# Local attention: the scores of both key blocks laid into one 128x128 matrix, and one transpose per query block and head instead of two

## The chip, the cores and the metric

The kernel runs on one core of one Trainium2 chip. The metric is the device time of one execution in microseconds; the median of three runs of the kernel before is 2232.43 us (2231.8 to 2232.46). A core has five engines that run their own instruction streams: TensorE (PE in the profile, its weight loads PEld), VectorE (DVE), ScalarE (ACT), GpSimd (POOL) and SyncE (SP). TensorE writes to PSUM only; VectorE and ScalarE read PSUM and SBUF; DMA queues move data between HBM and SBUF.

## The reference

One decoder layer on 2048 tokens of width 1024. A root-mean-square norm and one wide projection feed three branches: A, an RWKV-7 recurrence with 8 heads of 64; B, causal sliding-window attention with 8 query heads and 2 key/value heads of 64; C, cross-attention into 256 memory tokens. Each branch is gated, projected to 1024 and weighted by a sigmoid gate; the sum goes through an output projection and is added to the input. The change is in branch B, whose core is:

```
qb = q.reshape(bsz, nb, BLOCK, SW_KV_HEADS, SW_GROUP, SW_HEAD_DIM)    # BLOCK = WINDOW = 128
kband, vband = band(k), band(v)            # previous block of 128 keys, then the own block
s = einsum('bnqhgd,bnkhd->bnhgqk', qb, kband) * scale
rel = qi - kj + BLOCK                      # qi in 0..127, kj in 0..255
allowed = (rel >= 0) & (rel < WINDOW)      # and not the padding ahead of block 0
s = where(allowed, s, -1e30)
p = softmax(concatenate([s, sink]))[..., :-1]
o = einsum('bnhgqk,bnkhd->bnqhgd', p, vband)
```

For query qi of a block the allowed keys are those of the previous block with index above qi, and those of the own block with index up to qi. Of the 256 keys in the band exactly 128 are allowed, and each of the 128 column indices is allowed in exactly one of the two blocks (in the first block of the sequence the previous keys are padding).

## The kernel before

The tokens are worked in four blocks of 512 (`TB`), called blocks 0 to 3 here. In each block two generators are interleaved: `stream_r` (branch A: preparation, a triangular inverse on VectorE, a chain of small matmuls) and `stream_f` (cross-attention, then local attention by `swa_kv` and four calls of `swa_pair`, with gates and merges between). Then follow the merge of branch A and the output projection (`output`). Almost all of TensorE's time goes to dense projections, in which a float32 product is made of three float32r products of 128x512 (`gemm3`, lines 467 to 469, and lines 1222 to 1224 in `output`).

The order on each engine isn't the order in which the code is written. All instructions are recorded, and a list scheduler (`steps`, `lay_out`, `order`) places them engine by engine by rank, by estimated costs and by whether a buffer is free; buffers of one tag are taken in program order. The tag `g2` holds 128x512 float32 tiles, `NG` = 11 of them; PSUM has two buffers each of the tags `mm`, `rw` and `as_`, and one each of `oo` and `yps`.

`swa_pair(j, sb, ...)` treats two query heads and four query blocks of 128 tokens. It is called 16 times in all. Its steps:

- Scores (line 1136): for each query block and head, two matmuls of 128x256 (keys split into a high and a low part) into PSUM, the previous block's keys in columns 0 to 127 and the own block's in 128 to 255.
- Line 1140, on VectorE: adds the mask `amask` (0 or -1e30) to 128x256 scores, writes them to SBUF (`prs`) and takes the row's maximum. Eight per pair, each followed by a read of the accumulator.
- Line 1152, on ScalarE: exponential of 128x256 with the row's sum, eight per pair.
- Line 1164, on VectorE: the rows are scaled by the reciprocal sum, eight of 128x256.
- Line 1168: 128x128 transposes on TensorE into an `as_` tile, two for each query block and head, 16 per pair (14 in block 0, whose first query block has no previous keys). Line 1170, on ScalarE: copy of the 128x512 tile to SBUF, four per pair.
- Line 1178: value matmuls, for each query block, key block and head, 128 keys by 64 channels, into the `oo` tile.

`output` (lines 1214 to 1230) multiplies the merged sum by the output weights in two halves `n` of 512 columns. The sum's high parts are eight `g2` tiles (`split_acc`), which live until the second half is done. In each half four PSUM tiles `op[tt]` (two `mm`, two `as_`) collect 24 matmuls each. For each, a `g2` tile `xr` is loaded with the residual rows (line 1228, on ScalarE's DMA queue), line 1229 adds the product on VectorE, and line 1230 stores the tile (the same queue).

Of the kernel before, what the change touches and what calls it, by code (L numbers as in the profile page):

```python
# [9 lines left out]
F32 = mybir.dt.float32  # L10
F32R = mybir.dt.float32r
BF16 = mybir.dt.bfloat16
I32 = mybir.dt.int32
AF = mybir.ActivationFunctionType
# [6 lines left out]
NG = 11  # L21
# [286 lines left out]
def build(tc, A, nsb=4):  # L308
# [19 lines left out]
    def g2(dt=F32, shape=(128, TB)):  # L328
        return gp_.tile(list(shape), dt, name="g2")
# [9 lines left out]
    def s_ps():  # L339
        return ps.tile([128, 512], F32, name="as_", bufs=2)  # L340
# [54 lines left out]
    amask = bp.tile([128, 256], BF16, name="amask")  # L395
# [667 lines left out]
    vt = bp.tile([128, 5, 128], F32, name="Vt")  # L1063

    def swa_kv(sb, hT):
# [31 lines left out]
        S.activation(vt[:, 1:].rearrange("p a b -> p (a b)"), pt, AF.Copy)  # L1097

    def swa_pair(j, sb, hT, yh, yl):
# [29 lines left out]
        for b0 in (0, 2):  # L1129
            prs += [g2(shape=(128, 2, 256)) for _ in range(2)]  # L1130
            sp = [s_ps().rearrange("p (b k) -> p b k", b=2) for _ in range(2)]
            for b in (b0, b0 + 1):
                m0 = m0s[b]
                for i in range(2):
                    for n, kk in enumerate((kH, kL)):
                        PE.matmul(sp[i][:, b - b0, m0:], qs[i][:, b * 128:(b + 1) * 128], kk[:, g, b * 128 + m0:b * 128 + 256], start=n == 0, stop=n == 1)
            for b in (b0, b0 + 1):
                m0 = m0s[b]
                for i in range(2):
                    V.tensor_tensor_reduce(prs[b][:, i, m0:], sp[i][:, b - b0, m0:], amask[:, m0:], 1.0, -3e38, ALU.add, ALU.max, mx[:, b, i:i + 1])  # L1140
# [8 lines left out]
        for b in range(4):  # L1149
            m0 = m0s[b]  # L1150
            for i in range(2):
                S.activation(prs[b][:, i, m0:], prs[b][:, i, m0:], AF.Exp, scale=r2[:, b, i:i + 1], bias=mx[:, b, i:i + 1],  # L1152
                             accum_out=mx[:, b, 2 + i:3 + i])
# [6 lines left out]
        for b in range(4):  # L1160
            m0 = m0s[b]
            kb0 = m0 // 128
            for i in range(2):
                V.tensor_scalar(prs[b][:, i, m0:], prs[b][:, i, m0:], dn[:, b, i:i + 1], None, op0=ALU.mult)
            pt = s_ps().rearrange("p (a k q) -> p a k q", a=2, k=2)
            for i in range(2):
                for kb in range(kb0, 2):
                    PE.transpose(pt[:, i, kb], prs[b][:, i, kb * 128:(kb + 1) * 128], ident)
            P_ = g2(shape=(128, 2, 2, 128))
            last = S.activation(P_[:, :, kb0:], pt[:, :, kb0:], AF.Copy)  # L1170
            Ps.append(P_)
        ops_ = o_ps()
        prev = None
        for b in range(4):
            kb0 = m0s[b] // 128
            for kb in range(kb0, 2):
                for i, h in enumerate((EV, OD)):
                    m = PE.matmul(ops_[h, b * 128:(b + 1) * 128], vt[:, b + kb, g * 64:(g + 1) * 64], Ps[b][:, i, kb], start=kb == kb0, stop=kb == 1)  # L1178
                    behind(m, prev or last, not prev)
                    prev = m  # L1180
# [51 lines left out]
    def masks():  # L1232
        for t, n in ((gmask, "gmask"), (amask, "amask")):
            full = g2()[:, :t.shape[1]]
            nc.sync.dma_start(full, A[n])
            G.tensor_copy(t, full)
# [133 lines left out]
def host(inputs):  # L1370
# [30 lines left out]
    A["gmask"] = np.where(cI < 64, pI % 64 < cI, pI % 64 <= cI - 64).astype(f)  # L1401
    kj = np.arange(256)[None, :]
    A["amask"] = np.where((kj > pI) & (kj <= pI + 128), 0.0, -1e30).astype(f)
# [25 lines left out]
```

## Time and profile before

| | |
|---|---|
| median of three runs | 2232.43 us (2231.8 to 2232.46) |
| span of the profiled execution, first to last instruction | 2231.6 us |
| TensorE busy, weight loads busy | 2210.5 us (99%), 1798.2 us (81%) |
| VectorE busy | 1544.4 us (69%) |
| ScalarE busy | 920.2 us (41%) |
| GpSimd busy | 132.9 us (6%) |
| DMA moved | 433.17 MB, mean 194 GB/s |

The page gives the profiled execution's own time as its span alone; the three timed runs lie 0.2 to 0.9 us above it. The profile names an instruction by its source line, engine and operation, then output <- inputs, then the shapes. "Idle before" is the time in which an engine stood still ahead of an instruction, with the one that released it. A matmul's length includes its way through the array, so lengths of successive matmuls overlap; what one costs is read from the starts.

### The profile page before, as it was taken

To read this page: it belongs to the slowest core of one execution; us is meant where nothing else is said; L and a number is where in the kernel's file an instruction comes from. 1 tells how busy PE (TensorE), PEld (TensorE's weight loads), DVE (VectorE), ACT (ScalarE), POOL (GpSimd) and SP (SyncE) were. 2 spreads that over 40 slices of the span, in tenths; PEclk is the share of its full clock that TensorE was granted. 3 is DMA by queue.
4 is the path that set the end of the run, shared out by engine and by line. 5 is a ranking of instruction groups with operands and counts; after the bars stand their busy time and mean duration, and the time that the engine had idled before them with its cause. 6 is when DMAs were issued, how large, how long until landed. Compare 5 with 4: busy or idle time off the path is not lost. (4 is left out here: it accounts for less than half of the span.)

```text
span 2231.6 us, 36859 instructions
## 1 busy us (share of the span) xinstructions
PE 2210.5 (99%) x13682; PEld 1798.2 (81%) x13682; DVE 1544.4 (69%) x3993; ACT 920.2 (41%) x2042; POOL 132.9 (6%) x193
## 2 busy tenths in 40 slices
PE   8999999999999999999999999999999999999999
PEld 7888778778888778878888878877888887887887
DVE  7799699775479688943438958975245896896312
ACT  6664565445253355423215335432223434534210
POOL 1000010000000010000000001000000001000000
PEclk9999999999999999999999999999999999999999
DMA  6877556679845434446764534445675444344555
GB/s 218 293 240 258 186 183 217 224 274 351 313 163 167 143 133 158 146 169 231 243 237 143 178 125 150 144 142 199 222 254 198 162 156 156 119 151 132 201 196 189
DMA packets 149874, 433.17 MB, mean 194 GB/s; under 512 B 16704, under 2 KB 24256, under 8 KB 149696
## 3 DMA queue, kind: packets, MB, share of 16 engines
q1 hardware_dynamic: 133568, 401.45, 53.0%
q10 hardware_dynamic: 16128, 29.37, 3.9%
q8 instruction: 109, 1.79, 0.3%
q14 instruction: 69, 0.57, 0.1%
HBM read 334.81 MB, written 95.94 MB: 193 GB/s over the span
## 5 line engine op out<-in xcount | busy, mean ns | idle before, releaser
L467 PE MATMUL mm<-hH,whl 128*128 128x512 f32 x1888 | 752.4, 399 | 0.1
L469 PE MATMUL mm<-hH,whl 128*128 128x512 f32 x1888 | 750.2, 397 | 0.0
L468 PE MATMUL mm<-hL,whl 128*128 128x512 f32 x1888 | 745.3, 395 | 0.0
L469 PEld LDWEIGHTS mm<-hH,whl 128*128 128x128 f32 x1888 | 355.1, 188 | 71.8 <-issue 1.5
L467 PEld LDWEIGHTS mm<-hH,whl 128*128 128x128 f32 x1888 | 355.3, 188 | 68.7 <-DVE carry L677 0.4
L468 PEld LDWEIGHTS mm<-hL,whl 128*128 128x128 f32 x1888 | 355.3, 188 | 68.0 <-issue 0.9
L449 ACT ACTIVATE whl<-raw 128x512 fp32r<-128x512 f32 x178 | 111.3, 629 | 151.3 <-PE mm L469 95.1
L450 DVE TENSOR_TENSOR whl<-raw,whl 128x512 fp32r<-128x512 f32 x178 | 122.5, 691 | 48.2 <-ACT whl L449 45.9
L467 PE MATMUL mm<-yh,whl 128*128 128x512 f32 x384 | 151.9, 396 | 1.3 <-ACT gt L1190 0.8
L468 PE MATMUL mm<-yl,whl 128*128 128x512 f32 x384 | 151.1, 393 | 0.0
L469 PE MATMUL mm<-yh,whl 128*128 128x512 f32 x384 | 150.2, 391 | 0.0
L912 ACT ACTIVATE SP<-Z,Pl 64x64 f32<-64x64 f32 x256 | 76.4, 337 | 117.1 <-DVE Z L924 115.5
L819 DVE STREAM_SHUFFLE ibc<-Nc 128x496 f32<-128x496 f32 (+30 forms) x248 | 114.0, 473 | 0.0
L1205 DVE SCALAR_TENSOR_TENSOR g<-g,mm 128x512 f32<-128x512 f32 x32 | 21.8, 682 | 128.3 <-PE mm L469 128.3
L820 DVE TENSOR_TENSOR ibc<-ibc,Yi 128x496 f32<-128x496 f32 (+30 forms) x248 | 104.9, 423 | 4.1
L821 DVE TENSOR_TENSOR Yi<-Yi,ibc 128x496 f32<-128x496 f32 (+30 forms) x248 | 103.5, 418 | 1.2
L924 DVE SCALAR_TENSOR_TENSOR Z<-rw,Pl,SP 64x64 f32<-64x64 f32 x224 | 63.4, 283 | 40.6 <-PE rw L923 37.1
L1190 ACT ACTIVATE gt<-mm 128x512 f32<-128x512 f32 x64 | 37.9, 592 | 118.3 <-PE mm L469 118.2
L467 PEld LDWEIGHTS mm<-yh,whl 128*128 128x128 f32 x384 | 72.2, 188 | 16.9 <-ACT gt L1190 1.2
L468 PEld LDWEIGHTS mm<-yl,whl 128*128 128x128 f32 x384 | 72.2, 188 | 14.6
L1152 ACT ACTIVATE g<-g,mxs,st 128x256 f32<-128x256 f32 (+1 forms) x128 | 74.5, 584 | 22.8 <-DVE mxs L1145 22.6
L469 PEld LDWEIGHTS mm<-yh,whl 128*128 128x128 f32 x384 | 72.2, 188 | 14.4
(1847 smaller groups left out, 3804.7 us busy)
## 6 DMA issues: line engine op xcount, KB each, us to landing
whl<-k SPq DMA_DIRECT2D x486, 512.0 KB, 3.3
k<-whl SPq DMA_DIRECT2D x162, 512.0 KB, 4.3
raw<-in_w_in SPq DMA_DIRECT2D x118, 256.0 KB, 3.2
g<-in_x ACTq DMA_DIRECT2D x32, 256.0 KB, 4.9
out<-g ACTq DMA_DIRECT2D x32, 256.0 KB, 4.3
raw<-in_w_proj SPq DMA_DIRECT2D x24, 256.0 KB, 3.1
rt<-in_x ACTq DMA_DIRECT2D x24, 256.0 KB, 5.2
rt<-in_xt ACTq DMA_DIRECT2D x24, 256.0 KB, 5.5
```

Of the source, the lines that this page charges most:

```text
L449: S.activation(w[:, 0], raw, AF.Copy)
L450: V.tensor_tensor(w[:, 1], raw, w[:, 0].bitcast(F32), op=ALU.subtract)
L467: PE.matmul(out, lh, rh, start=i == 0, stop=False)
L468: PE.matmul(out, lh, rl, start=False, stop=False)
L469: PE.matmul(out, ll, rh, start=False, stop=i == n - 1)
L819: V.stream_shuffle(bc[:, :, :w], N_[:, :, s + 1:], [s] * 32)
L820: V.tensor_tensor(bc[:, :, :w], bc[:, :, :w], Y[:, :, s:s + 1].to_broadcast([128, n, w]), op=ALU.mult)
L821: V.tensor_tensor(Y[:, :, s + 1:], Y[:, :, s + 1:], bc[:, :, :w], op=ALU.add)
L912: S.activation(SP[h, i], Z[h, i, e, c], AF.Copy, scale=g[4][h, c:c + 1])
L924: upds = [V.scalar_tensor_tensor(Sst[h, g[0]] if c == NC_ - 1 else Z[h, i, e, c + 1], pS[h, i, e], g[4][h, c:c + 1], SP[h, i], op0=ALU.mul ...
L1152: S.activation(prs[b][:, i, m0:], prs[b][:, i, m0:], AF.Exp, scale=r2[:, b, i:i + 1], bias=mx[:, b, i:i + 1], accum_out=mx[:, b, 2 + i:3 + i])
L1190: S.activation(t, gp, AF.Tanh, scale=0.5)
```

## The change

The scores are made as before. ScalarE then copies the previous block's half (128 columns of two query blocks at once) into an SBUF tile, and VectorE lays the own block's half over it by a predicated copy with the mask `upto` (column index up to the row). The result is one 128x128 matrix per query block and head that holds every allowed score and no other. For the first query block of the sequence the previous half is filled with -1e30 by GpSimd instead. The row's maximum is taken by a reduction of its own, for two query blocks at once. Exponentials are 128x128, the scaling works on two query blocks at once, and there is one transpose per query block and head.

Since keys of both blocks now share a column, the values need a correction. ScalarE copies the transposed matrix (`both`), VectorE multiplies it by the mask `over`, which keeps only the previous block's part (`prev`). The value product is `both` times the own block's values plus `prev` times `vd`, the previous block's values less the own block's. The number and size of the value matmuls stay. `vd` is made once per block in `swa_kv`. It takes 2 KB per partition, as much as one `g2` tile, and `NG` goes from 11 to 10. The masks come from one array instead of two.

```diff
-NG = 11
+NG = 10
...
-    amask = bp.tile([128, 256], BF16, name="amask")
+    upto = bp.tile([128, 128], U8, name="upto")
+    over = bp.tile([128, 128], BF16, name="over")
...
+    vd = bp.tile([128, 4, 128], F32, name="Vd")
...
+        b = 0 if sb else 1
+        V.tensor_tensor(vd[:, b:], vt[:, b:4], vt[:, b + 1:], op=ALU.subtract)
...
         for b0 in (0, 2):
-            prs += [g2(shape=(128, 2, 256)) for _ in range(2)]
+            P_ = g2(shape=(128, 2, 2, 128))
+            prs.append(P_)
...
-            for b in (b0, b0 + 1):
-                m0 = m0s[b]
-                for i in range(2):
-                    V.tensor_tensor_reduce(prs[b][:, i, m0:], sp[i][:, b - b0, m0:], amask[:, m0:], 1.0, -3e38, ALU.add, ALU.max, mx[:, b, i:i + 1])
+            k0 = 1 if m0s[b0] else 0
+            if k0:
+                G.memset(P_[:, :, 0], -1e30)
+            for i in range(2):
+                S.activation(P_[:, i, k0:], sp[i][:, k0:, :128], AF.Copy)
+                V.copy_predicated(P_[:, i], upto.unsqueeze(1).to_broadcast([128, 2, 128]), sp[i][:, :, 128:])
+                V.tensor_reduce(mx[:, b0:b0 + 2, i], P_[:, i], axis=AX.X, op=ALU.max)
...
         for b in range(4):
-            m0 = m0s[b]
             for i in range(2):
-                S.activation(prs[b][:, i, m0:], prs[b][:, i, m0:], AF.Exp, scale=r2[:, b, i:i + 1], bias=mx[:, b, i:i + 1],
-                             accum_out=mx[:, b, 2 + i:3 + i])
+                P_ = prs[b // 2][:, i, b % 2]
+                S.activation(P_, P_, AF.Exp, scale=r2[:, b, i:i + 1], bias=mx[:, b, i:i + 1], accum_out=mx[:, b, 2 + i:3 + i])
...
-        for b in range(4):
-            m0 = m0s[b]
-            kb0 = m0 // 128
+        for b0 in (0, 2):
+            P_ = prs[b0 // 2]
             for i in range(2):
-                V.tensor_scalar(prs[b][:, i, m0:], prs[b][:, i, m0:], dn[:, b, i:i + 1], None, op0=ALU.mult)
-            pt = s_ps().rearrange("p (a k q) -> p a k q", a=2, k=2)
+                V.tensor_tensor(P_[:, i], P_[:, i], dn[:, b0:b0 + 2, i:i + 1].to_broadcast([128, 2, 128]), op=ALU.mult)
+            pt = s_ps().rearrange("p (i b q) -> p i b q", i=2, b=2)
             for i in range(2):
-                for kb in range(kb0, 2):
-                    PE.transpose(pt[:, i, kb], prs[b][:, i, kb * 128:(kb + 1) * 128], ident)
-            P_ = g2(shape=(128, 2, 2, 128))
-            last = S.activation(P_[:, :, kb0:], pt[:, :, kb0:], AF.Copy)
-            Ps.append(P_)
+                for b in range(2):
+                    PE.transpose(pt[:, i, b], P_[:, i, b], ident)
+            both = g2(shape=(128, 2, 2, 128))
+            last = S.activation(both, pt, AF.Copy)
+            prev = g2(shape=(128, 2, 2, 128))
+            last2 = V.tensor_tensor(prev.rearrange("p i b q -> p (i b) q"), pt.rearrange("p i b q -> p (i b) q"), over.unsqueeze(1).to_broadcast([128, 4, 128]), op=ALU.mult)
+            Ps.append((both, prev))
...
-            for kb in range(kb0, 2):
+            for u in range(2 - kb0):
                 for i, h in enumerate((EV, OD)):
-                    m = PE.matmul(ops_[h, b * 128:(b + 1) * 128], vt[:, b + kb, g * 64:(g + 1) * 64], Ps[b][:, i, kb], start=kb == kb0, stop=kb == 1)
-                    behind(m, prev or last, not prev)
+                    w = (vt[:, b + 1], vd[:, b])[u]
+                    m = PE.matmul(ops_[h, b * 128:(b + 1) * 128], w[:, g * 64:(g + 1) * 64], Ps[b // 2][u][:, i, b % 2], start=not u, stop=u == 1 - kb0)
+                    if prev:
+                        behind(m, prev)
+                    else:
+                        behind(m, last, True)
+                        behind(m, last2, True)
```

The scheduler lays the whole program out anew. Three places follow, line numbers of the changed kernel being some 10 higher. First TensorE at the last pair of block 1: transposes (line 1168 before, 1175 now; `g` tiles hold the probabilities) among the dense matmuls of a gate. Before, down to half of the pair's transposes:

```order
L1168 MATMUL as__10234<-c_ident,g_9986 128x128 x4
L1168 MATMUL as__10243<-c_ident,g_9987 128x128 x2
L469 MATMUL mm<-hH,whl 128x512
L467 MATMUL mm<-hH,whl 128x512
L468 MATMUL mm<-hL,whl 128x512
L1168 MATMUL as__10243<-c_ident,g_9987 128x128 x2
```

Now, all of the pair's transposes:

```order
L1175 MATMUL as__10167<-c_ident,g_9917 128x128 x2
L469 MATMUL mm<-hH,whl 128x512
L1175 MATMUL as__10167<-c_ident,g_9917 128x128 x2
L1175 MATMUL as__10178<-c_ident,g_9934 128x128 x2
L470 MATMUL mm<-hL,whl 128x512
L1175 MATMUL as__10178<-c_ident,g_9934 128x128 x2
```

Eight transposes stand here in place of sixteen. Behind the last of them come eleven dense matmuls, and then the pair's first value matmul (seven before).

Second, TensorE in block 3's output stage, where the second half begins. `as__22002` and `mm` are the second half's first tiles, `as__22004` its fourth (`g_21718`, `g_21739` and so on are the high parts of the sum, in order). Before:

```order
L1222 MATMUL mm<-whl,g_21781 128x512
L1223 MATMUL mm<-whl,g_21781 128x512
L1224 MATMUL mm<-whl,mB 128x512
L1222 MATMUL as__22002<-whl,g_21781 128x512
L1223 MATMUL as__22002<-whl,g_21781 128x512
L1224 MATMUL as__22002<-whl,mB 128x512
L1222 MATMUL as__22004<-whl,g_21718 128x512
```

Now `as__21827` is the second tile and `as__21829` the fourth; `g_21543` is the first high part, `g_21627` the fifth, and an `mm` with `g_21543` in this place is the third tile:

```order
L1238 MATMUL mm<-whl,mB 128x512
L1236 MATMUL as__21827<-whl,g_21627 128x512
L1237 MATMUL as__21827<-whl,g_21627 128x512
L1236 MATMUL mm<-whl,g_21543 128x512
L1237 MATMUL mm<-whl,g_21543 128x512
L1238 MATMUL mm<-whl,mB 128x512
L1236 MATMUL mm<-whl,g_21564 128x512
L1236 MATMUL as__21829<-whl,g_21543 128x512
```

Before, three tiles run ahead and 33 matmuls of the second half stand ahead of the fourth tile's first one. Now two tiles run ahead, and 29 matmuls stand ahead of the third tile's first one. Blocks 1 and 2 have the same order here; in block 0 all 48 matmuls of the first two tiles stand ahead.

Third, the same stage on ScalarE's queue, which issues the loads of the residual rows and the stores. Before:

```order
L1228 DMA g_21985<-in_x 128x512
L1228 DMA g_21989<-in_x 128x512
L1228 DMA g_21993<-in_x 128x512
L1230 DMA out<-g_21985 128x512
L1230 DMA out<-g_21989 128x512
L1230 DMA out<-g_21993 128x512
L1228 DMA g_21997<-in_x 128x512
```

Now:

```order
L1242 DMA g_21810<-in_x 128x512
L1242 DMA g_21814<-in_x 128x512
L1244 DMA out<-g_21810 128x512
L1244 DMA out<-g_21814 128x512
L1242 DMA g_21818<-in_x 128x512
L1242 DMA g_21822<-in_x 128x512
```

Three row blocks of the first half were loaded ahead of the first store, and two are now; the third and fourth stand behind two stores.

More of the change, by code (lines that the diff above doesn't have):

```diff
@@ L13 @@
 I32 = mybir.dt.int32
+U8 = mybir.dt.uint8
 AF = mybir.ActivationFunctionType
@@ L1232, in masks @@
     def masks():
[L1233 to L1236, printed above, removed]
+        full = g2()[:, :384]
+        nc.sync.dma_start(full, A["gmask"])
+        for i, t in enumerate((gmask, upto, over)):
+            G.tensor_copy(t, full[:, i * 128:(i + 1) * 128])
     def x_norm(sb):
@@ L1400, in host @@
     pI, cI = np.arange(128)[:, None], np.arange(128)[None, :]
-    A["gmask"] = np.where(cI < 64, pI % 64 < cI, pI % 64 <= cI - 64).astype(f)
-    kj = np.arange(256)[None, :]
-    A["amask"] = np.where((kj > pI) & (kj <= pI + 128), 0.0, -1e30).astype(f)
+    A["gmask"] = np.concatenate([np.where(cI < 64, pI % 64 < cI, pI % 64 <= cI - 64), cI <= pI, pI > cI], axis=1).astype(f)
     A["bones"] = (pI // 64 == np.arange(2)[None, :]).astype(f)
```

## The prediction

> **What bounds the kernel now.** I read the page first, for the engine that has no slack. "PE", "DVE" are busy tenths in 40 slices of 55.8 us.
>
> ```profile
> span 2231.6 us, 36859 instructions
> ...
> PE 2210.5 (99%) x13682; PEld 1798.2 (81%) x13682; DVE 1544.4 (69%) x3993; ACT 920.2 (41%) x2042; POOL 132.9 (6%) x193
> ...
> PE   8999999999999999999999999999999999999999
> ...
> DVE  7799699775479688943438958975245896896312
> ...
> L469 PE MATMUL mm<-hH,whl 128*128 128x512 f32 x1888 | 750.2, 397 | 0.0
> ```
>
> TensorE is busy 99% and its commonest matmul is never kept waiting (the last column, 0.0). VectorE has 687 us of idle time in the mean, but not everywhere: its digits reach 9 in the first block. So I asked for busy time by stretch, in the first block's attention pairs:
>
> ```profile
> core 0: us, PE busy (x) PEld busy (x) DVE busy (x) ACT busy (x) POOL busy (x), PEclk, DMA share, GB/s
> ...
> 312.00:360.00 48.00, 47.66 (x279) 39.01 (x278) 45.24 (x110) 29.84 (x68) 2.34 (x2) 1.00 0.59 202
> 360.00:410.00 50.00, 49.12 (x280) 40.29 (x279) 49.42 (x159) 27.38 (x62) 2.72 (x2) 1.00 0.66 224
> ```
>
> From 312 to 410 us VectorE is full too (94 and 99%) while TensorE is at 99 and 98%. There, and only there, an added VectorE operation may have no cover.
>
> Busy time of a pipelined engine proves little alone, since records overlap. The timeline of TensorE in block 1 shows whether a transpose displaces other work (columns: start, length, engine, line, operation):
>
> ```profile
> 898.96 0.40 PE L469 MATMUL mm<-hH,whl 128*128 128x512 f32 x1
> 899.19 0.60 PE L1168 MATMUL as__9694<-c_ident,g 128*128 128x128 f32 x4
> 899.63 0.60 PE L1168 MATMUL as__9703<-c_ident,g 128*128 128x128 f32 x4
> 899.99 0.48 PE L467 MATMUL mm<-hH,whl 128*128 128x512 f32 x1
> 900.30 0.39 PE L468 MATMUL mm<-hL,whl 128*128 128x512 f32 x1
> 900.53 0.39 PE L469 MATMUL mm<-hH,whl 128*128 128x512 f32 x1
> ```
>
> From the last dense matmul ahead of eight transposes (898.96) to the third behind (900.53) pass 1.57 us. Three dense steps, at 0.227 us each (worked out below from 33 rows), are 0.68 us. The eight transposes took the other 0.89 us, 0.111 us each, and pushed the dense stream back by all of it. They are on the path.
>
> The Trainium skill (Perfetto Trace Analysis, Identifying the Most-Contended Engine) says that matmul busy time is a poor measure of how near TensorE is to its limit, and the busy share of LDWEIGHTS a better one. By that the 81% in the row would leave slack in which transposes might be free; the timeline above speaks against it, and the case has a chance of its own below.
>
> **The change part by part.** *Transposes.* The row of line 1168 over the whole span and its row for block 0 (PE busy and count, then weight loads):
>
> ```profile
> 0.00:2231.60 2231.60, 38.32 (x248) 28.56 (x248) 1.00 0.57 194
> ...
> 200.00:420.00 220.00, 8.95 (x56) 6.86 (x56) 1.00 0.62 211
> ```
>
> 248 now. Afterwards each of 16 pairs has two tiles of four, 128. The 120 that go are worth 120 x 0.111 = 13.4 us, of which block 0 has 56 - 32 = 24, or 2.7 us. Score matmuls (line 1136) and value matmuls (line 1178) keep their number and size; only their operands change.
>
> The Trainium skill (TensorE: Matmul & The Clock Gate, Part 4) gives about 275 ns for a transpose inside a kernel; by that the 120 would be worth 33 us and the estimate 2202 us. The starts above show 0.111 us each, so I do not use it.
>
> *VectorE.* Rows of the operations that go, and the nearest ones to those that come:
>
> ```profile
> L1140 DVE CUSTOM_DVE_ANT_0 g<-as__3269,amask x2: 285/352/420, 285.6 to 285.8; 128x128 f32<-128x128 f32 x1, 128x256 f32<-128x256 f32 x1
> ...
> L1140 DVE DVE_READ_ACCUMULATOR2_ANT mxs<- 128x1 f32 x128 | 10.5, 82 | 0.0
> ...
> L1164 DVE TENSOR_SCALAR g<-g,dns 128x256 f32<-128x256 f32 x120 | 34.1, 348 | 0.2
> ...
> L892 DVE TENSOR_TENSOR rt<-rt,st 128x256 f32<-128x256 f32 x32 | 12.4, 420 | 0.4
> ...
> L1182 DVE TENSOR_TENSOR g<-oo,g 128x512 f32<-128x512 f32 x16 | 10.9, 682 | 0.1
> ```
>
> A pair loses eight mask-and-maximum operations (420 + 82 ns) and eight scalings (348 ns): 6.8 us. It gains four predicated copies, four maxima over 256 elements and four products of 256 (420 ns each by line 892), and two products of 512 from PSUM (682 ns): 4.7 us and the four copies. The trace has no predicated copy. Below it lies the 128-element row, 0.285 us; above, two passes over 256, 0.84 us. I take 0.42 us, the 256-element operation on the same PSUM tile with a mask. A pair then needs 6.4 us, 0.4 us less than now; at 0.84 it needs 8.1, 1.3 us more. Four value differences of up to 512 elements (0.69 us by the same row) are 2.7 us in all. Over the kernel that is -4 to +24 us on an engine with 687 us idle, hidden by TensorE's own stream. Without that cover, in block 0, the dear copy costs 4 x 1.3 + 0.5 = 5.7 us; the cheap one nothing.
>
> *ScalarE.*
>
> ```profile
> L1152 ACT ACTIVATE g<-g,mxs,st 128x256 f32<-128x256 f32 x120 | 70.6, 591 | 20.6 <-DVE mxs L1145 20.5
> ...
> L1152 ACT ACTIVATE g<-g,mxs,st 128x128 f32<-128x128 f32 x8 | 3.9, 487 | 2.2 <-DVE mxs L1145 2.1
> ...
> L1170 ACT ACTIVATE g<-as__2913 x1: 383/383/383, 263.9 to 263.9; 128x256 f32<-128x256 f32 x1
> L1170 ACT ACTIVATE g<-as__2920 x1: 598/598/598, 264.6 to 264.6; 128x512 f32<-128x512 f32 x1
> ```
>
> Eight exponentials shrink from 591 to 487 ns (-0.8 us), four 512-copies become two (-1.2 us), four 256-copies come (+1.5 us): -0.5 us a pair on an engine at 41%. Nothing on the path.
>
> *New waits.* The first value matmul now waits for the copy on ScalarE and for the product on VectorE. Everything on TensorE is queued behind it, but eleven dense matmuls stand ahead of it in the order of block 1's last pair (2.5 us), against some 0.7 us for the product: covered. The memsets on GpSimd (four, block 0) and the one mask load that goes are hidden by an engine at 6% and by the warm-up.
>
> *One g2 buffer less (NG 11 to 10).* I looked for the place where the ring is full. It is the output stage: eight high parts of the merged sum stay until the second half is done, so three slots were left for the residual rows `xr`, and two are now. Lines 1229 and 1228/1230:
>
> ```profile
> L1229 DVE SCALAR_TENSOR_TENSOR g<-as__6298,g x1: 692/692/692, 580.1 to 580.1; 128x512 f32<-128x512 f32 x1
> L1229 DVE SCALAR_TENSOR_TENSOR g<-as__6300,g x1: 691/691/691, 590.1 to 590.1; 128x512 f32<-128x512 f32 x1
> ...
> L1229 DVE SCALAR_TENSOR_TENSOR g<-as__11580,g x1: 692/692/692, 1121.0 to 1121.0; 128x512 f32<-128x512 f32 x1
> L1229 DVE SCALAR_TENSOR_TENSOR g<-as__11582,g x1: 691/691/691, 1129.0 to 1129.0; 128x512 f32<-128x512 f32 x1
> ...
> L1229 DVE SCALAR_TENSOR_TENSOR g<-as__16782,g x1: 692/692/692, 1663.8 to 1663.8; 128x512 f32<-128x512 f32 x1
> L1229 DVE SCALAR_TENSOR_TENSOR g<-as__16784,g x1: 692/692/692, 1671.4 to 1671.4; 128x512 f32<-128x512 f32 x1
> ...
> L1229 DVE SCALAR_TENSOR_TENSOR g<-as__21870,g x1: 692/692/692, 2204.2 to 2204.2; 128x512 f32<-128x512 f32 x1
> L1229 DVE SCALAR_TENSOR_TENSOR g<-as__21872,g x1: 692/692/692, 2212.3 to 2212.3; 128x512 f32<-128x512 f32 x1
> ```
>
> ```profile
> 2205.36 0.39 PE L1222 MATMUL mm<-whl,g 128*128 128x512 f32 x1
> ...
> 2212.61 0.39 PE L1224 MATMUL as__22002<-whl,mB 128*128 128x512 f32 x1
> 2213.05 0.50 PE L1222 MATMUL as__22004<-whl,g 128*128 128x512 f32 x1
> ```
>
> ```profile
> DMA to landing us min/median/max: 2.6/4.9/9.4
> ...
> DMA to landing us min/median/max: 2.0/4.3/8.3
> ```
>
> In each pair the second and the fourth row block are added. The fourth comes 10.0, 8.0, 7.6 and 8.1 us behind the second: it waits until the first block's store has landed and its own row has been loaded into that slot (medians 4.9 us for a load, 4.3 us for a store). TensorE meanwhile runs the other three tiles ahead: 33 matmuls from 2205.36 to 2212.61 (32 steps, 0.227 us each), then 0.2 us of waiting, and the fourth tile's first matmul 0.75 us behind its sum. With two slots the third row block makes that round trip as well. In the new order 29 matmuls of two tiles (6.58 us) stand ahead of the third tile's first one. It is due 2205.36 + 6.58 = 2211.94, which is 7.74 us after the second sum; it can start 0.75 us behind the third sum, at 8.75, 8.35 and 8.85 us in blocks 1 to 3. The waits are 1.0, 0.6 and 1.1, together 2.7 us; in block 0, where 48 matmuls stand ahead (10.9 + 1.16 = 12.1 us against 10.75), none. The fourth sum follows 0.7 us later and its tile is due 0.9 us later, so today's waits there (0.2 in the last block, 0.1 in block 1 by the same sum) go. Net cost 2.4 us; bounds 0 (a shorter trip) and, with each trip as long as block 0's, 3 x 3.0 - 0.3 = 8.7 us.
>
> *Sum.* 2231.6 - 13.4 + 2.4 = 2220.6 us of span. The median of the runs shown, 2232.43, lies 0.8 us above the profiled span, so 2221.4 us.
>
> **The rivals.** *VectorE becomes the bound in block 0.* For it: 94 and 99% there. Against it: TensorE lost under 1 us in each of the two stretches, and a copy at 0.42 us makes the pairs lighter. It needs the copy near 0.84 us and costs the 5.7 us above: 2227.1 us.
>
> *The transposes only fill gaps* that other waits leave. For it: the 81%. Against it: the run at 899 us, where the dense stream is dense on both sides. Then nothing is gained, the freed time returns as waiting, and 2232 to 2235 us results.
>
> *The row trip in the output stage decides: slower than before.* The place is the third tile's first matmul in blocks 1 to 3. If store and load take their longest (8.3 and 9.4 us) with 0.7 for the sum, the trip is 18.4 us and the wait 18.4 + 0.75 - 7.74 = 11.4 us a block, 34 us: 2253 us. It decides from 13.4 / 3 = 4.5 us a block, a trip over 11.5 us. Against it: four trips in the trace lie between 7.6 and 10.0 us.
>
> That the change doesn't remove the transposes is excluded by the order: two to eight in a row, 128 in all.
>
> **How the numbers follow.** Forecast 0.74 (2221.4 us, own range 2217 to 2225); block 0's VectorE 0.12; gaps 0.08; row trip 0.06. The range is 2216 to 2228 us: it holds the first two cases, the low end being no output wait (2219.0) and some 3 us fewer short waits ahead of the transposes, the high end the dear copy. About 0.2% (4.5 us) is what a measurement of this kernel tells from no change: faster needs under 2228 us. That is the forecast and most of the second case, 0.85; within 0.2% most of the gap case and the rest of the second, 0.09; slower 0.06.
>
> **What would show it.** PE instructions fall by 120 to 13562 and PE busy time by about as much as the span. In the groups, line 1175 has 128 transposes at about 0.111 us start to start. COPY_PREDICATED shows near 0.42 us; 0.8 or more would put the second case forward, with TensorE waits on VectorE between 250 and 410 us. In the output stage two sums, not three, come together, then a gap of about 8 us to the third, with a TensorE wait of about 1 us for the third (line 1236 for line 1243). The forecast is wrong if the span falls by under 7 us or over 15 us, or if the dense stream shows new waits elsewhere.

## The result

The changed kernel takes 2219.73 us (median of five runs, 2217.62 to 2222.35); the kernel before, beside it, 2232.08 us. The ratio is 0.9945, with a 95% interval of 0.9933 to 0.9957: 12.4 us less. In a later comparison it took 2218.43 us, ratio 0.9946 (0.9934 to 0.9959). The forecast was 2221.4 us.

### The profile page after: what moved, and what is told of

It reads as the page before. It is cut to its first block, busy times and chain, and to the rows that moved or that the text cites. A ratio compares the mean times of both kernels' runs of the same rounds, so it can differ in the third digit from the quotient of the medians.

```text
span 2217.8 us, 36497 instructions
## 1 busy us (share of the span) xinstructions
PE 2197.4 (99%) x13562; PEld 1790.3 (81%) x13562; DVE 1549.5 (70%) x3837; ACT 912.8 (41%) x2074; POOL 134.3 (6%) x198
## 4 chain that ended last, share of the span: by engine, by line
PE 91%; DVE 5%; ACT 1%; DMA 1%; POOL 1%; issue 1%; SPq 0%; DVEq 0%; POOLq 0%; ACTq 0%
PE mm L471 22%; PE mm L469 22%; PE mm L470 22%; PE rw L925 1%; PE mm L1236 1%; PE oo L1188 1%; PE mm L1237 1%; PE mm L1238 1%; PE rw L901 1%; PE rw L916 1%; PE rw L771 1%; PE yps L881 1%; PE yps L877 1%; PE rw L788 1%; PE oo L771 1%
## 5 line engine op out<-in xcount | busy, mean ns | idle before, releaser
L1219 DVE SCALAR_TENSOR_TENSOR g<-g,mm 128x512 f32<-128x512 f32 x32 | 21.8, 681 | 127.4 <-PE mm L471 127.4
L1243 DVE SCALAR_TENSOR_TENSOR g<-mm,g 128x512 f32<-128x512 f32 x16 | 11.1, 692 | 118.9 <-PE mm L1238 75.6
L471 PEld LDWEIGHTS mm<-yh,whl 128*128 128x128 f32 x384 | 72.2, 188 | 14.2 <-issue 0.2
L922 DVE TENSOR_TENSOR Z<-rw,dk 64x128 f32<-64x128 f32 x128 | 36.9, 288 | 57.7 <-PE rw L916 41.7
```

The source lines that it names most:

```text
L471: PE.matmul(out, ll, rh, start=False, stop=i == n - 1)
L922: upd = V.tensor_tensor(Z[h, :n, e, c], pu[h], dk[h, :n, c:c + 1].to_broadcast([64, n, C]), op=ALU.mult)
```

## The profile after

The page of the changed kernel, its first rows:

```profile
span 2217.8 us, 36497 instructions
...
PE 2197.4 (99%) x13562; PEld 1790.3 (81%) x13562; DVE 1549.5 (70%) x3837; ACT 912.8 (41%) x2074; POOL 134.3 (6%) x198
...
DVE  7799799875479779953438958975145895896412
```

TensorE has 120 instructions fewer and 13.1 us less busy time (2210.5 before), and the span is 13.8 us shorter (2231.6 before). TensorE is as full as it was. VectorE has 5 us more, ScalarE 7.4 us less.

The transposes, now line 1175, over the whole span (the window runs past the end at 2217.8 us; TensorE busy and count, then weight loads), and in the timeline of block 1, where eight of them stand together:

```profile
0.00:2231.60 2231.60, 22.07 (x128) 16.70 (x128) 1.00 0.58 194
```

```profile
895.42 0.39 PE L471 MATMUL mm<-hH,whl 128*128 128x512 f32 x1
895.66 0.60 PE L1175 MATMUL as__9639<-c_ident,g 128*128 128x128 f32 x4
896.09 0.60 PE L1175 MATMUL as__9650<-c_ident,g 128*128 128x128 f32 x4
896.45 0.48 PE L469 MATMUL mm<-hH,whl 128*128 128x512 f32 x1
896.76 0.40 PE L470 MATMUL mm<-hL,whl 128*128 128x512 f32 x1
896.99 0.39 PE L471 MATMUL mm<-hH,whl 128*128 128x512 f32 x1
```

From 895.42 to 896.99 pass 1.57 us for three dense steps (0.68 us) and eight transposes, as in the trace of before: a transpose still costs 0.111 us.

The new operations on VectorE: the first rows of line 1148, and the groups of lines 1149 and 1171 (busy, mean ns of one, idle before):

```profile
L1148 DVE COPY_PREDICATED g<-upto,as__2654 x1: 426/426/426, 205.0 to 205.0; 128x256 f32<-128x256 uint8 x1
L1148 DVE COPY_PREDICATED g<-upto,as__2655 x1: 442/442/442, 208.0 to 208.0; 128x256 f32<-128x256 uint8 x1
```

```profile
L1149 DVE TENSOR_REDUCE mxs<-g 128x2 f32<-128x256 f32 x64 | 24.7, 410 | 0.2
L1171 DVE TENSOR_TENSOR g<-g,dns 128x256 f32<-128x256 f32 x64 | 24.1, 416 | 0.3
```

The output stage, line 1243 (line 1229 before), in blocks 1 and 3, with what ended VectorE's idle time:

```profile
1115.13 0.69 DVE L1243 SCALAR_TENSOR_TENSOR g<-as__11499,g 128x512 f32<-128x512 f32 x1
1122.32 0.69 DVE L1243 SCALAR_TENSOR_TENSOR g<-mm,g 128x512 f32<-128x512 f32 x1 [6.49 <-DMA g<-in_x]
...
2189.90 0.69 DVE L1243 SCALAR_TENSOR_TENSOR g<-as__21695,g 128x512 f32<-128x512 f32 x1
2197.73 0.69 DVE L1243 SCALAR_TENSOR_TENSOR g<-mm,g 128x512 f32<-128x512 f32 x1 [7.14 <-DMA g<-in_x]
```

```profile
2198.48 0.50 PE L1236 MATMUL mm<-whl,g 128*128 128x512 f32 x1 [0.69 <-DVE g L1243]
```

Two sums come together and the third waits for its row, as forecast. The gap is 7.2 us in block 1 and 7.8 in block 3, and only block 3 shows a TensorE wait for it, 0.7 us. In the second profile of this kernel (experiment 7) block 1 has such a wait, 0.6 us, and block 3 has none.

Block 0 shows something that the prediction does not have. First TensorE's longest waits between 190 and 560 us (us in total, times, longest); then two stretches around 308.6 us (from and to, length, busy time and count of TensorE, its weight loads, VectorE, ScalarE and GpSimd, then the granted clock, the DMA share and GB/s):

```profile
PE rw L788 <- DVE QE L779: 1.5, 1, 1.5
PE rw L901 <- DVE Z L926: 1.2, 1, 1.2
PE rw L788 <- ACT BK L789: 0.7, 1, 0.7
```

```profile
305.20:308.60 3.40, 1.24 (x12) 0.67 (x8) 3.37 (x7) 0.60 (x2) 0.00 (x0) 1.00 0.96 314
308.60:315.40 6.80, 6.21 (x20) 4.66 (x21) 6.46 (x15) 5.28 (x12) 0.00 (x0) 0.50 0.10 41
```

TensorE worked for 1.24 of 3.4 us, and then its clock was halved for 6.8 us. In the kernel before it worked more in the same stretch and kept its clock:

```profile
305.20:308.60 3.40, 2.72 (x20) 1.78 (x16) 3.37 (x7) 3.40 (x12) 0.00 (x0) 1.00 0.83 275
308.60:315.40 6.80, 5.82 (x29) 4.12 (x30) 6.67 (x21) 6.51 (x19) 0.00 (x0) 1.00 0.32 118
```

**Gain by block.** For the experiments I use one more measure: the start of the last 128x512 matmul of each block (numbers 1974, 3947, 5920 and 7893 of 7894, counted from 0; the dense work is the same in every kernel but the two with filling matmuls) in the trace of before, minus its start in the other trace. The differences from block to block, in us:

| kernel | block 0 | block 1 | block 2 | block 3 | sum |
|---|---|---|---|---|---|
| changed | 2.3 | 3.6 | 5.0 | 2.9 | 13.7 |
| changed, a second profile | 2.9 | 2.9 | 4.8 | 4.3 | 15.0 |
| before, NG = 10 | -0.9 | 0.0 | 1.3 | -0.2 | 0.2 |
| before, one transpose left out | -0.2 | 0.8 | 1.6 | 2.0 | 4.3 |
| the same, shorter copies | 3.3 | 3.5 | 4.7 | 3.5 | 15.0 |
| the same, shorter scaling | 1.5 | 1.4 | 2.9 | 2.7 | 8.4 |
| the same, 128 keys | 4.1 | 2.7 | 4.6 | 4.2 | 15.6 |
| changed, transposes doubled | 3.6 | -0.2 | 1.2 | 0.6 | 5.2 |
| changed, copies doubled | -2.6 | 2.8 | 4.1 | 3.1 | 7.4 |

The two profiles of the changed kernel tell how far a single block may be trusted: they differ by up to 1.4 us.

## The experiments

The theory: the 120 transposes lay on TensorE's path, 0.111 us each; VectorE hides the rest; the smaller ring costs some waits in the output stage. The rivals: VectorE is the bound in block 0, or transposes only fill gaps.

**1. Only the ring made smaller.** In the kernel before:

```diff
-NG = 11
+NG = 10
```

> The kernel before with one g2 buffer less (10 for 11) and nothing else. My forecast's term: +2.4 us, three waits of about 1, 0.6 and 1.1 us at the third tile of the output stage in blocks 1 to 3, so about 2234.5 us. From the profile of the changed kernel, where the time won falls by only 0.7 us across the output stages: +0.7 us, about 2232.8 us. Rival, the ring also starves other stages: over +3 us (2235 and more), with TensorE waits outside the output stage.

Measured: 2233.81 us, ratio 1.0006 (0.9997 to 1.0015). That is 1.2 us, between -0.7 and 3.3; the blocks of its profile sum to 0.2 us, and TensorE waits for the residual sums once, 0.3 us (line 1222). The smaller ring costs little, and 2.4 us was at the upper half of what it may cost.

**2. Only the transposes taken away.** In the kernel before, the previous key block's weights are not transposed; its value matmuls use the own block's weights in their place, so the output is not the reference's:

```diff
-                for kb in range(kb0, 2):
-                    PE.transpose(pt[:, i, kb], prs[b][:, i, kb * 128:(kb + 1) * 128], ident)
+                PE.transpose(pt[:, i, 1], prs[b][:, i, 128:], ident)
...
-            last = S.activation(P_[:, :, kb0:], pt[:, :, kb0:], AF.Copy)
+            last = S.activation(P_[:, :, kb0:], pt[:, :, 1:].to_broadcast([128, 2, 2 - kb0, 128]), AF.Copy)
```

> The kernel before, in which the previous key block's 120 transposes are left out (the copy behind them reads the own block's transposes twice, so that the attention output is not the reference's); masks, copies, buffers and value matmuls are as before. If TensorE is the path and a transpose costs 0.111 us: 2232.1 - 13.4 = 2218.7 us. If transposes only fill gaps: 2231 to 2232 us. If the dense part of block 0 is set by VectorE, the 22 to 24 transposes of block 0 give nothing there and 2221.4 us results.

Measured: 2227.72 us, ratio 0.9979 (0.9970 to 0.9988): 4.9 us, not 13.4. The step of the prediction that this run was to confirm fails in it. Its transposes did become cheaper: start to start they take 10.3 us in place of 25.7. But 11 us of that came back. TensorE's waits account for 5.8 of them (21.8 us in all, 16.0 before) and a halved clock for at most 3.4; the rest is not accounted for. Three of its waits in block 1 (in total, times, longest), which the kernel before does not have:

```profile
PE mm L467 <- DVE carry L677: 0.9, 1, 0.9
PE mm L1221 <- DVE g L1204: 0.5, 1, 0.5
PE rw L801 <- DVE carry L677: 0.4, 1, 0.4
```

and the two for `carry` stand again in blocks 2 and 3, the other one in block 2. In block 0 it waited 2.9 us once and then ran at half clock:

```profile
PE mm L467 <- DVE dns L1154: 2.9, 1, 2.9
...
305.40:308.80 3.40, 1.19 (x8) 0.74 (x8) 3.27 (x6) 3.40 (x12) 0.00 (x0) 0.99 0.34 58
308.80:315.60 6.80, 5.45 (x17) 4.36 (x18) 5.89 (x20) 5.18 (x14) 0.00 (x0) 0.50 0.28 110
```

So "TensorE's time is worth its face value" needed a second condition: whoever it next waits for must be early enough. Experiments 8 to 10 follow this up.

**3. The transposes of the changed kernel doubled.**

```diff
-                    PE.transpose(pt[:, i, b], P_[:, i, b], ident)
+                    for _ in range(2):
+                        PE.transpose(pt[:, i, b], P_[:, i, b], ident)
```

> The changed kernel with each of its 128 transposes made twice into the same place. TensorE as the path: +128 x 0.111 = 14.2 us, 2219.7 + 14.2 = 2233.9 us. Gap theory: no change, 2220 us. If block 0 is set by VectorE: its 32 are hidden, +10.7 us, 2230.4 us.

Measured: 2232.05 us, ratio 0.9996 (0.9987 to 1.0005), 12.3 us above the changed kernel (11.8 or 12.5 if each is taken against the kernel before beside it). At face value 128 x 0.111 = 14.2 us. In blocks 1 to 3 of its profile 9.9 us are lost (11.4 gained by the changed kernel, 1.5 by this one) for 96 x 0.111 = 10.7. "Transposes only fill gaps" falls with this. For block 0 the profile shows no price: it gains 1.3 us over the changed kernel, with 32 transposes more. But the profiled execution is the fastest of the ten and the only one with a mean granted clock of 1.000, so block 0 stays open here.

**4. The predicated copies of the changed kernel doubled** (64 more, 0.44 us each, 28 us of VectorE).

```diff
-                V.copy_predicated(P_[:, i], upto.unsqueeze(1).to_broadcast([128, 2, 128]), sp[i][:, :, 128:])
+                for _ in range(2):
+                    V.copy_predicated(P_[:, i], upto.unsqueeze(1).to_broadcast([128, 2, 128]), sp[i][:, :, 128:])
```

> The changed kernel with each of the 64 predicated copies made twice (0.44 us each by the changed kernel's profile): 27.9 us more on VectorE, 7.0 of them in block 0. My theory: hidden in blocks 1 to 3, where VectorE has idle time; in block 0, where VectorE is over 94% busy from 312 to 410 us, between nothing and all 7.0 us: 2219.7 to 2226.7 us, 2223 as the likeliest, with block 0 alone later. Rival, VectorE sets the pairs everywhere: +28 us, 2247 us.

Measured: 2225.56 us, ratio 0.9969 (0.9957 to 0.9981), 5.8 us above the changed kernel. By the table 4.9 us of it are in block 0, whose 16 added copies take 7.0 us, and 1.4 us in the other three, whose 48 take 21.1 us. VectorE had no cover in block 0 and nearly full cover elsewhere, as the prediction had it; a copy of 0.84 us would have cost in block 0 about what was written for it (5.7 us).

**5. Block 0 relieved of VectorE work.** In the changed kernel, block 0 scales its weights on ScalarE:

```diff
-                V.tensor_tensor(P_[:, i], P_[:, i], dn[:, b0:b0 + 2, i:i + 1].to_broadcast([128, 2, 128]), op=ALU.mult)
+                if sb:
+                    V.tensor_tensor(P_[:, i], P_[:, i], dn[:, b0:b0 + 2, i:i + 1].to_broadcast([128, 2, 128]), op=ALU.mult)
+                else:
+                    for b in range(2):
+                        S.activation(P_[:, i, b], P_[:, i, b], AF.Copy, scale=dn[:, b0 + b, i:i + 1])
```

> The changed kernel, in block 0 with the scaling of the probabilities on ScalarE (32 copies of 128x128 with a scale) instead of VectorE (16 products of 128x256, 0.416 us): VectorE has 6.7 us less in block 0, ScalarE some 10 more on an engine with 38 to 50% idle there. If VectorE sets block 0 and its stall at 307 us lets the clock fall: the clock stays at full speed, 2.5 to 5 us are won, 2215 to 2217 us. If TensorE alone sets block 0: 2219.7 us. If ScalarE becomes late instead: 2221 us and more.

Measured: 2221.36 us, ratio 0.9953 (0.9939 to 0.9966). Nothing was won; block 0 gains 0.6 us against 2.3 in the changed kernel, and the half clock stays (from 308.7 us). TensorE now waited for other things in block 0, a value matmul for VectorE (1.6 us) and transposes for ScalarE's scaling (0.6 and 0.3 us). Moving work off a full engine did not pay. The new waits lie on the chain from scores to value matmuls, which the move probably lengthened; no run tests that alone.

**6. The residual rows out of the ring.** In the changed kernel:

```diff
-                xr = g2()
+                xr = rt_()
```

> The changed kernel with the residual rows of the output stage in the tag rt (six tiles) instead of g2, so that no row block waits for a store. If the trip of the row blocks still costs what the profile of the changed kernel shows (0.7 us over all blocks): 2219.0 us. If it costs the forecast's 2.4 us: 2217.3 us. Rival, the rt tiles are missed by the next block's first steps: 2221 us or more. The clock reduction seen in block 0 at 308 us should stay, since block 0's order ahead of the output stage is not touched.

Measured: 2218.15 us, ratio 0.9936 (0.9924 to 0.9949), 1.6 us below the changed kernel. The wait of line 1236 for the residual sum is gone from its profile. The two intervals overlap, and the changed kernel's later run (2218.43 us) is only 0.3 us slower, so it is not shown that this version is the faster one. The changed kernel with eleven ring buffers was not tried: it doesn't fit into SBUF.

**7. The wait ahead of the half clock filled.** In the changed kernel, six matmuls of no use ahead of the transposes of line 788 in the pair that waited at 307 us; alone, together with the edit of experiment 6, and the changed kernel again beside them:

```diff
+        if sb == 0 and p == 2:
+            busy = mm_ps().rearrange("p (a b) -> p a b", a=4)
+            prev = ms[-1]
+            for _ in range(6):
+                m = PE.matmul(busy, onesw, onesw.unsqueeze(1).to_broadcast([128, 4, 128]), start=True, stop=True)
+                behind(m, prev)
+                prev = m
```

> The changed kernel with six matmuls of 128x512 of no use (1.36 us) put on TensorE ahead of the transposes of line 788 that waited 1.54 us at 307 us in block 0, just before the granted clock fell to 0.5 for 6.83 us. Theory A, the waiting lets the clock fall, and the half clock costs up to 3.4 us: no stretch at 0.5 behind the fill, TensorE time won, 2216.3 to 2218.5 us. Theory B, the stretch costs nothing, since block 0 follows VectorE there: 2219.5 to 2221 us, whatever the clock shows. Theory C, the clock falls for another reason: the stretch at 0.5 stays at the same place, 2219.5 to 2221 us.

> The changed kernel with the residual rows of the output stage in tag rt (2218.15 us alone) and with the six filling matmuls of the run before. If the two gains are independent: theory A of the filled wait gives 2214.5 to 2217 us, theories B and C 2217.5 to 2219.5 us.

> The changed kernel itself, on the same chip as the other runs of this call. Both theories: 2218 to 2221.5 us, with a stretch at clock 0.5 of 6.83 us near 309 us.

Measured: 2232.95 us (ratio 1.0007, 0.9998 to 1.0016), 2231.96 us (1.0002, 0.9993 to 1.0011) and 2218.43 us. The fill cost 14.5 us, and no theory had that. The stretch from 285 to 303 us, columns as above, first with the fill, then in the changed kernel beside it:

```profile
285.00:303.00 18.00, 7.48 (x45) 6.50 (x44) 14.53 (x32) 9.08 (x26) 0.00 (x0) 0.50 0.00 0
```

```profile
285.00:303.00 18.00, 18.00 (x90) 14.80 (x91) 16.95 (x36) 12.33 (x32) 0.00 (x0) 1.00 0.77 261
```

By the kernel's text and the timeline, the filling matmuls took one of the two PSUM banks `mm`, through which the dense projections go in the order of their allocation. The projections behind them had to wait for the fill, and the fill was tied behind a step at 302 us: TensorE stood empty where it had had 16 us of dense work, DMA too, and the clock was halved for 20.5 us. As a test of what the halved clock costs this run is of no use; the edit moved more than it filled.

**8. The kernel of experiment 2 with 128 keys a query block.** Mask, maximum, exponentials and scaling leave the previous key block out:

```diff
-                    V.tensor_tensor_reduce(prs[b][:, i, m0:], sp[i][:, b - b0, m0:], amask[:, m0:], 1.0, -3e38, ALU.add, ALU.max, mx[:, b, i:i + 1])
+                    V.tensor_tensor_reduce(prs[b][:, i, 128:], sp[i][:, b - b0, 128:], amask[:, 128:], 1.0, -3e38, ALU.add, ALU.max, mx[:, b, i:i + 1])
...
-                V.tensor_scalar(prs[b][:, i, m0:], prs[b][:, i, m0:], dn[:, b, i:i + 1], None, op0=ALU.mult)
+                V.tensor_scalar(prs[b][:, i, 128:], prs[b][:, i, 128:], dn[:, b, i:i + 1], None, op0=ALU.mult)
```

> The kernel before, without the previous block's 120 transposes (as in the experiment that leaves these out, 2227.72 us) and now also without the previous block in mask, maximum, exponentials and scaling: 128 keys a query block in place of 256, so the output is not the reference's. VectorE is spared about 8 x (0.420 - 0.285) us in the masks and some 8 x 0.15 us in the scalings, 2.3 us a pair. Theory A, the missing part of the 13.4 us became waits of TensorE for a VectorE that is late (1.03 + 0.51 + 0.26 us in each of blocks 1 to 3, 5.4 us in all): they go, about 2222.3 us. Theory B, the waits come from the order of the work and not from VectorE's load: they stay, 2226.5 to 2228.5 us.

Measured: 2218.30 us, ratio 0.9945 (0.9931 to 0.9958), 13.2 us below before: the whole price of the transposes, and more than theory A gave. Of the waits for `carry` one of 0.2 us is left, and block 0 has no half clock. But this edit makes ScalarE's exponentials shorter too, so two more runs take the engines apart.

**9. The same with only ScalarE's copy shorter**, and **10. with only VectorE's scaling shorter** (experiment 2 and one edit each):

```diff
-            last = S.activation(P_[:, :, kb0:], pt[:, :, 1:].to_broadcast([128, 2, 2 - kb0, 128]), AF.Copy)
+            last = S.activation(P_[:, :, 1], pt[:, :, 1], AF.Copy)
...
-                    m = PE.matmul(ops_[h, b * 128:(b + 1) * 128], vt[:, b + kb, g * 64:(g + 1) * 64], Ps[b][:, i, kb], start=kb == kb0, stop=kb == 1)
+                    m = PE.matmul(ops_[h, b * 128:(b + 1) * 128], vt[:, b + kb, g * 64:(g + 1) * 64], Ps[b][:, i, 1], start=kb == kb0, stop=kb == 1)
```

> The kernel before without the previous block's 120 transposes, and with the copy of the weights from PSUM cut to the own block (256 elements for 512; the value matmuls of the previous block use the own block's weights, so the output is not the reference's). ScalarE is spared 4 x (0.600 - 0.383) = 0.9 us a pair, about what the run with 128 keys spared it; VectorE does all of its work. Theory A, a late VectorE took the rest of the gain: about 2227.7 us as without the cut, 2226 to 2229. Theory B, ScalarE was the late one: 2218 to 2222 us, as with 128 keys.

```diff
-                V.tensor_scalar(prs[b][:, i, m0:], prs[b][:, i, m0:], dn[:, b, i:i + 1], None, op0=ALU.mult)
+                V.tensor_scalar(prs[b][:, i, 128:], prs[b][:, i, 128:], dn[:, b, i:i + 1], None, op0=ALU.mult)
```

> The kernel before without the previous block's 120 transposes, and with the scaling of the weights on VectorE cut to the own 128 keys (0.280 for 0.348 us, eight a pair, 0.5 us a pair); masks, maxima, exponentials and copies as before; the output is not the reference's. Theory A, a late VectorE took the rest of the gain: 0.5 us is part of the 1.8 us that is waited for in a block, so some of the waits go, 2222 to 2227 us. Theory B, ScalarE was the late one: 2227.7 us, 2226.5 to 2229.

Measured: 2217.81 us, ratio 0.9929 (0.9913 to 0.9946), and 2225.11 us, ratio 0.9967 (0.9954 to 0.9980). By these numbers, theory B (ScalarE was late) is the nearer one for the first (0.2 us under its range) and theory A (VectorE was late) holds for the second; neither stands as it was put. VectorE's timeline tells why. In experiment 2, the stretch ahead of the copy of `carry` that TensorE waits for in block 1:

```profile
832.13 0.42 DVE L1140 CUSTOM_DVE_ANT_0 g<-as__8919,amask 128x256 f32<-128x256 f32 x1
...
840.21 0.42 DVE L1140 CUSTOM_DVE_ANT_0 g<-as__8936,amask 128x256 f32<-128x256 f32 x1
...
842.41 0.14 DVE L677 COPY carry<-mm 128x1 f32<-128x1 f32 x1
```

All eight masks of a pair, from 832.13 to 840.21 us, stand ahead of it, VectorE is full (14.74 of the 15 us from 828), and TensorE's bank `mm` comes free when that copy is done. In experiment 9:

```profile
834.59 0.42 DVE L1140 CUSTOM_DVE_ANT_0 g<-as__8919,amask 128x256 f32<-128x256 f32 x1
834.93 0.08 DVE L1140 DVE_READ_ACCUMULATOR2_ANT mxs<- 128x1 f32 x1
834.93 0.15 DVE L677 COPY carry<-mm 128x1 f32<-128x1 f32 x1
```

One mask stands ahead, seven behind. VectorE does the same work in both kernels (1544.6 and 1542.8 us busy); the order that the scheduling laid down is another, though the edit did not touch VectorE. In experiment 8 all eight masks are ahead again, but shorter (0.28 us), and the copy starts at 835.11 us without a TensorE wait. In experiment 10 all eight are ahead at full length, and part of the waits stays (0.4 us in each block, for 0.9 in blocks 1 to 3 of experiment 2). In the changed kernel two predicated copies stand in the 14 us ahead of it, and the maxima come behind:

```profile
825.64 0.44 DVE L1148 COPY_PREDICATED g<-upto,as__8922 128x256 f32<-128x256 uint8 x1
826.57 0.43 DVE L1148 COPY_PREDICATED g<-upto,as__8923 128x256 f32<-128x256 uint8 x1
...
839.33 0.16 DVE L679 COPY carry<-mm 128x1 f32<-128x1 f32 x1
...
839.59 0.41 DVE L1149 TENSOR_REDUCE mxs<-g 128x2 f32<-128x256 f32 x1
```

So the waits for `carry` are VectorE's, by its load or by its order, and which order results is set anew by every edit. They are 3.7 of the 10.4 us between experiments 2 and 9. By the table 3.4 us of the difference are in block 0, where TensorE waited once for VectorE (2.9 us, above) and once for ScalarE (1.3 us) and the clock fell; what each of these is worth is not shown. What isn't settled either is which feature of an edit makes the scheduling choose the good order: experiment 9 spares ScalarE 0.9 us a pair and changes what the value matmuls read, and no run takes these apart. Nor did a run price the halved clock by itself.

## Why the prediction was right, and where it was not

**Transposes: -13.4 us.** The price, 0.111 us, stands in the trace after, and experiment 3 gives 87% of it back, though its profile shows none of that in block 0. The blocks gained 2.3 us (forecast 2.7) and 11.4 us (forecast 3 x 3.55 = 10.7, less the output waits). The step that fails is a silent one: that with the 120 gone, everything else stays where it is. Experiment 2 took the same 120 away and got 4.9 us; its copy of `carry` became the next thing waited for. By its timeline the changed kernel was spared because its maxima came behind that copy; no run tests this order by itself. That the sum came out within 2 us of the measurement is owed to that as well as to the price, and that part is luck: the working had not looked at it.

**Output stage: +2.4 us.** The mechanism is right, two sums and then a gap, but the term was mis-sized: 0.7 us of waiting in block 3, none in blocks 1 and 2. The working took the old gaps (8.0, 7.6 and 8.1 us) for the trip; they are now 7.2, 6.9 and 7.8. With the 0.75 us from a sum to its tile's first matmul that is 7.9, 7.6 and 8.6, against 7.74 us of work ahead. Stores landed sooner in this profile:

```profile
g<-in_x ACTq DMA_DIRECT2D x32, 256.0 KB, 4.6
out<-g ACTq DMA_DIRECT2D x32, 256.0 KB, 3.3
```

3.3 us in the median for 4.3 before, 4.6 for a load in place of 4.9. With trip and cover within a microsecond of each other, a difference of 1 us a block decided between a wait and none; the lower bound, 0, was the better guess. Experiment 1 (1.2 us, interval -0.7 to 3.3) and experiment 6 (1.6 us) allow 0.7 and 2.4 alike.

**VectorE, ScalarE: 0.** The predicated copy was taken as 0.42 us and measures 0.426 to 0.457. VectorE's sum, forecast at -4 to +24 us, is +5.1; ScalarE's, forecast at -8 us, is -7.4. The rival "VectorE the bound in block 0" was sound in its mechanism and its price (experiment 4: 4.9 us in block 0 for the 5.7 written); it did not come because the copy is cheap. That an added VectorE operation lacks cover "there, and only there", from 312 to 410 us, was too narrow. The trace of before has VectorE as full in block 1, in the stretch in which experiment 2 then waited for `carry`:

```profile
828.00:843.00 15.00, 14.95 (x100) 12.35 (x100) 14.76 (x38) 4.18 (x8) 0.00 (x0) 1.00 0.33 107
```

**New waits: 0.** Right for the value matmuls, wrong as a whole. The prediction named new waits in the dense stream as a sign against it, and there are some: 1.5 and 0.7 us at 307 us, with half a clock behind them, and 0.8 us each in blocks 1 and 3 (line 944 for line 941). Others went: TensorE's waits sum to 16.0 us before and 16.1 after.

**Transposes fill gaps; the row trip decides.** Both are out: experiment 3 for the first, the gaps of 7.2 to 7.8 us, against the 11.5 from which it would decide, for the second.

## What to carry to other kernels

On a full engine an instruction's price is its start-to-start time inside a dense run, not its share of busy time; but removing it is worth that price only if what the engine waits for next is early, so look at what the second-fullest engine has ahead of the operations that free buffers. Where a scheduler lays the order, an edit's own worth is a price plus or minus a re-laid order, here from 4.9 to 15.3 us in four variants that removed the same 120 instructions; run the edit in two or three variants before saying what it is worth. Filling an idle stretch with dummy work must take no buffer that real work takes in turn.

## What the runs showed of the hardware

The prediction says nothing of the granted clock. In block 0, near 308 us, it fell to half after stretches of 3.4 us in which TensorE had worked 1.2 us (the changed kernel, experiment 2), 1.5 (experiment 4, the changed kernel's second profile), 1.6 (experiment 6), 1.9 (experiment 1) or 2.5 us (experiment 5), and stayed there for 3.4 or 6.8 us; behind the hole of experiment 7 it stayed for 20.5 us. It did not fall in experiment 9, whose least busy 3.4 us near there hold 1.58 us. Experiment 9, and then the stretch ahead of the fall in experiment 5:

```profile
304.90:308.30 3.40, 1.58 (x10) 0.89 (x9) 3.31 (x6) 3.40 (x11) 0.00 (x0) 1.00 0.49 195
308.60:315.40 6.80, 6.41 (x34) 4.87 (x33) 6.61 (x22) 6.58 (x18) 0.00 (x0) 1.00 0.33 116
```

```profile
305.30:308.70 3.40, 2.52 (x12) 1.37 (x12) 3.37 (x6) 3.35 (x11) 0.00 (x0) 1.00 0.75 266
```

So busy time has no sharp threshold in these runs. The Trainium skill (TensorE: Matmul & The Clock Gate, Part 1) describes a free-running activity window of about 3.4 us; the lengths seen here, once, twice and six times that, agree. The clock's changes in these traces lie on such a grid: in the changed kernel it came back at 21.85 us and fell at 308.57 us, 84 times 3.413 us later. Where a stretch lies on that grid explains only part: the grid's window holds 1.72 us in experiment 9, without a fall, but 1.96 in experiment 1 and 2.54 in experiment 5, with one.

What sorts these windows better is the kind of work. Without the 128x128 transposes, TensorE was busy for 0 to 0.61 us in the seven windows behind which the clock fell near 308 us, and for 0.86 us or more in those behind which it did not. In experiment 5 all the matmuls of the window are transposes. Against it stand the second kernel of experiment 7, whose clock fell behind 1.37 us of other work, and the falls in the first 20 us of most of these kernels, which do not follow it. No edit varied this, so it is a reading of a few windows and not shown.

The Trainium skill (TensorE: Matmul & The Clock Gate, Why this matters for your kernels) advises against idle gaps of TensorE above about 3 us. Here shorter ones were not safe: the longest single gap ahead of the changed kernel's fall is 1.5 us.

What the halved clock costs is only bounded. At most it is half of 6.8 us, 3.4 us. In experiment 3 the executions differ in their clock: four with a mean granted clock of 0.999 or more took 2229.4 us in the median, six with 0.998 took 2232.9. That difference, 3.5 us, is a correlation over ten executions and was not brought about by an edit. In the kernel before, a mean clock of 0.998 in place of 0.999 went with 0.8 us more in one comparison (27 executions) and 1.6 us in another (20).
